# Latent heads: a pair's projection may come one pair sooner, more tiles for its operands, even filling

## The chip, the cores and the metric

The kernel runs on one core of a Trainium2 chip, in one launch. The metric is the device time of an execution in microseconds (us). Five engines work beside each other, each through its own queue and in the order of that queue: TensorE (PE; its weight loads are listed as PEld), VectorE (DVE), ScalarE (ACT), GpSimd (POOL) and SyncE (SP), which here issues nearly all loads.

## The reference, cut

One encoder layer over 512 positions of width 2048, all float32:

```
mod = silu(c) @ w_ada + b_ada                  # six rows: shift, scale, gate, twice
h   = rms_norm(x) * (1 + sc1) + sh1
proj = h @ w_in                                # q, k, v of 8 differential heads; cq (512), ckv (256), k_pe (64)
a   = softmax(q1 k1 + bias) - lam * softmax(q2 k2 + bias)     # per differential head, q and k normed
a_out = rms_norm(a @ v) * (1 - lambda_init)
q_m = rms_norm(rms_norm(cq) @ w_q_b)           # 8 latent heads of 128 + 64, rotary on the 64
kv  = rms_norm(ckv) @ w_kv_b                   # k_nope (128) and v (128) of each latent head
k_m = rms_norm([k_nope, k_pe])                 # rotary on the 64
b_out = softmax(q_m k_m) v
x = x + gt1 * ([a_out, b_out] @ w_out)
x = x + gt2 * ((silu(h2 @ w_gate) * (h2 @ w_up)) @ w_down)    # h2 = second norm and modulation of x
```

## The kernel before

A float32 matmul is done as three matmuls of halves: each operand is split into a high part (`hi`) and a rest (`lo`), and hi·hi, hi·lo and lo·hi are summed in PSUM (L242, L243, L244). Splitting a weight block takes a cast on ScalarE (L90) and a subtraction (L98) on VectorE or on GpSimd, which take turns.

Four stages follow each other: the input modulation and the first part of the input projection (0 to 200 us), the eight differential heads (to 542 us), the eight latent heads (to 755 us), and then the output projection, the second norm and the feed-forward part, whose code the diff leaves alone.

TensorE runs its instructions in the order in which the program is written; a scheduler places those of the other engines around them. The heads are written out step by step by two strings: `DIFF_STEPS` for a differential head, `MLA_STEPS` for a latent one (`s` scores of a block of 128 queries, `t` transposes of the softmax, `v` products with v, `o` operands of the next head, `e` the transposes of a finished head's outputs, `F` filler). At an `F`, `between()` takes matmuls from a generator, `projections()` (L979), for so many microseconds, and a piece of the sums of the modulation (`side`). The numbers are `DIFF_FILL` (per differential head, in eight parts) and `MLA_FILL` (per latent head, in four parts).

`projections()` gives, in this order: the input projection for the later differential heads and for the latents; then for each pair of latent heads `mla_project(pr)` (48 matmuls with `w_q_b`, here QB: L242 to L244 with `cqh`/`cql`, and 24 with `w_kv_b`, KVB: with `ckvh`/`ckvl`); behind pairs 1 and 3 half an output projection, `out_half` (matmuls into `ps_o`). Behind each pair it stops until the first head of this pair has been started and the last differential head's outputs exist (L995). Where it stops, an `F` gives nothing.

What a pair's projection brings along on the other engines: copies of the query tiles out of PSUM (`qm`, L840), sums of squares (L859, L872), and on GpSimd the rotary part of four query tiles (L792 to L795, L854), their statistics (L861 to L863), the key statistics (L880, L261, L262) and eight scalings of key tiles (`kn` L884, `kpt` L886). The last thing a differential head does on GpSimd is four times, for each block of 128 queries, the norm of its output: `zs` (L766 to L768) and `z` (L769). `finish()` transposes the four z on TensorE (L775) at the `e` of the next head; for differential head 7 that is the `e` of latent head 0, behind the first scores of that head.

`dup_tile` gives the tiles for `qpe` and `kpt` (eight buffers: four of each, one pair), `split_v` and `vr` share the tag `v` (eight buffers). `ada` tiles (L308) hold the loads for the modulation's sums; all these loads are issued by SyncE in order.

Of the kernel before, what the change touches and what calls it, by code (L numbers as in the profile page):

```python
# [10 lines left out]
F32 = mybir.dt.float32  # L11
F32R = mybir.dt.float32r
# [6 lines left out]
P = 128  # L19
# [4 lines left out]
H = 8  # L24
# [175 lines left out]
def hybrid_layer(ctx, tc, a, out):  # L200
    nc = tc.nc
# [62 lines left out]
    sh = open_pool("sh")  # L264
# [320 lines left out]
    for i, (k0, nk) in enumerate(BLOCKS):  # L585
        final = i + 1 == len(BLOCKS)
        for h in range(1 if final else FIRST):
            tag = next_tag()
# [20 lines left out]
    wk = open_pool("wk")  # L609
# [13 lines left out]
    def dup_tile(name):  # L623
        return sh[1].tile([P, 2, 2, 64], F32, tag="dup", bufs=8, name=name)

    def split_v(src, own=False):
        vv = (wk if own else sh)[1].tile([P, 2, P], F32R, tag="v", bufs=2 if own else 8, name="v")
        act.copy(out=vv[:, 0, :], in_=src)
        dve.tensor_tensor(out=vv[:, 1, :], in0=src, in1=f(vv)[:, 0, :], op=ALU.subtract)
        return vv  # L630
# [44 lines left out]
    mixT = [None] * KC  # L675
# [166 lines left out]
    def mla_project(pr):  # L842
# [23 lines left out]
        kn, kp, v = [], [], []  # L866
        rk = sm(2 * NT, "rsk", 2)
        for t in range(NT):
            pv = pss[t].rearrange("p (h s n) -> p h s n", h=2, s=2)
            sq = wk[1].tile([P, 384], F32, tag="sq", bufs=2, name="sqm")[:, :256].rearrange("p (a b) -> p a b", a=2)  # L870
            act.activation(sq, pv[:, :, 0, :], AF.Square)
            dve.tensor_reduce(out=rk[:, 2 * t:2 * t + 2], in_=sq, axis=AX.X, op=ALU.add)  # L872
            vr = sh[1].tile([P, 2, P], F32, tag="v", bufs=8, name="vr")
            act.copy(out=vr, in_=pv[:, :, 1, :])
            v.append(vr)
            k = raw_tile("kn")[:, :256].rearrange("p (h n) -> p h n", h=2)
            copy(K_ACT[t], k, pv[:, :, 0, :])
            kn.append(k)
# [101 lines left out]
    def projections():  # L980
# [10 lines left out]
        for pr in range(4):  # L991
            yield from mla_project(pr)
            if pr in (1, 3):
                yield from out_half({1: 2, 3: 3}[pr])
            while pr not in started or mixT[H - 1] is None:  # L995
                yield 0
# [477 lines left out]
DIFF_STEPS = "s0 F s1 n F t0 F e s2 v0 F t1 F s3 v1 F t2 F o0 v2 t3 F o1 v3 F"  # L1474
DIFF_FILL = (26.0, 26.0, 26.0, 26.0, 26.0, 26.0, 26.0, 26.3)
DIFF_SIDE = (1, 2, 1, 2, 1, 2, 1, 1)
# [3 lines left out]
MLA_STEPS = "s0 F t0 e F1 t1 s1 v0 F t2 F1 v1 t3 s2 F v2 F1 o0 v3 F o2 o3 s3 o1 F1"  # L1480
MLA_FILL = (16.0, 15.7, 16.0, 0.2, 14.1, 19.0, 3.3, 12.8)

# [37 lines left out]
```

## Time and profile before

| | |
|---|---|
| median of 3 runs | 2257.24 us (2250.57 to 2259.51) |
| the profiled execution | 2254.27 us, of which its span 2252.5 us |
| mean granted clock of TensorE | 0.996 |
| TensorE busy | 2178.6 us, 97% of the span |
| its weight loads | 2000.5 us, 89% |
| VectorE busy | 1648.1 us, 73% |
| ScalarE busy | 942.6 us, 42% |
| GpSimd busy | 262.7 us, 12% |

All rows below are of the profiled execution, in microseconds from the start of its span. A row of the timeline gives start, duration, engine, line, operation, out<-in and shapes; in brackets how long the engine had been idle before, and what ended that.

### The profile page before, as it was taken

Reading aid. Unit: us, or ns where it says so; the run is one execution under the profiler, and the core shown is the slowest. Engines: PE = TensorE matmul, PEld = TensorE weight load, DVE = VectorE, ACT = ScalarE, POOL = GpSimd, SP = SyncE. Lnnn points to the kernel's source line nnn. Section 1 sums busy time; section 2 is a strip of 40 time slices with the busy share of each in tenths; the row PEclk is TensorE's granted clock in tenths of the full one; section 3 lists DMA queues with packets and bytes.
Section 4 is the critical chain, followed back from the end, with each engine's and each line's share of the span. In section 5 each row is a group of like instructions: output and inputs, shape, how many; then the busy total and the mean of one; then the engine's idle time right before and its main releaser. Section 6 shows DMA issues by size and latency. Waiting matters only on the chain.

```text
span 2252.5 us, 35369 instructions
## 1 busy us (share of the span) xinstructions
PE 2178.6 (97%) x13906; PEld 2000.5 (89%) x13906; DVE 1648.1 (73%) x2362; ACT 942.6 (42%) x1567; POOL 262.7 (12%) x408
## 2 busy tenths in 40 slices
PE   3899999998989999999999999999999999999999
PEld 3899998998777788899999999999999888888887
DVE  5997888868988687867777777777777677443554
ACT  4434555566555334534444444444444522221221
POOL 0003444345554000000000000000000000000000
PEclk9999999999999999999999999999999999999999
DMA  9995355422442684523333333333334686333443
GB/s 284 302 292 169 83 154 158 134 87 86 158 139 96 247 295 159 159 85 118 117 118 117 132 122 122 114 118 116 122 123 131 219 296 224 99 127 99 154 149 103
DMA packets 270826, 345.00 MB, mean 153 GB/s; under 512 B 15005, under 2 KB 171142, under 8 KB 270530
## 3 DMA queue, kind: packets, MB, share of 16 engines
q1 hardware_dynamic: 267864, 338.18, 46.5%
q10 hardware_dynamic: 2794, 4.55, 0.5%
q8 instruction: 109, 1.79, 0.3%
q14 instruction: 59, 0.48, 0.1%
HBM read 322.71 MB, written 19.96 MB: 152 GB/s over the span
## 4 chain that ended last, share of the span: by engine, by line
PE 67%; DVE 1%; DMA 0%; ACT 0%; issue 0%; POOL 0%; SPq 0%; DVEq 0%
PE ps_d L243 7%; PE ps_d L244 7%; PE ps_d L242 7%; PE ps_X L1285 5%; PE ps_X L1283 5%; PE ps_X L1284 5%; PE ps_W L1285 3%; PE ps_W L1283 3%; PE ps_W L1284 3%; PE ps_Y L1285 2%; PE ps_Z L1285 2%; PE ps_o L242 2%; PE ps_o L244 2%; PE ps_o L243 2%; PE ps_Y L1283 2%; PE ps_Z L1283 2%
## 5 line engine op out<-in xcount | busy, mean ns | idle before, releaser
L90 ACT CAST hi<-raw 128x1024 fp32r<-128x1024 f32 (+2 forms) x228 | 221.2, 970 | 479.2 <-PE ps_d L243 262.7
L98 DVE TENSOR_TENSOR lo<-raw,hi 128x1024 fp32r<-128x1024 f32 (+2 forms) x215 | 242.6, 1129 | 217.3 <-ACT hi L90 213.5
L1266 ACT CAST wh<-wr 128x1024 fp32r<-128x1024 f32 x160 | 168.2, 1051 | 245.3 <-PE ps_X L1284 69.2
L1285 PE MATMUL ps_X<-comb,wl 128*128 128x256 f32 x960 | 269.4, 281 | 0.0
L1283 PE MATMUL ps_X<-comb,wh 128*128 128x256 f32 x960 | 268.6, 280 | 0.0
L1284 PE MATMUL ps_X<-comb,wh 128*128 128x256 f32 x960 | 267.1, 278 | 0.0
L1249 DVE TENSOR_TENSOR wl<-wr,wh 128x1024 fp32r<-128x1024 f32 x160 | 195.6, 1222 | 76.5 <-ACT wh L1266 76.2
L244 PE MATMUL ps_d<-lo,ax 128*128 128x512 f32 x640 | 249.0, 389 | 0.0
L243 PE MATMUL ps_d<-hi,ax 128*128 128x512 f32 x640 | 249.0, 389 | 0.0
L242 PE MATMUL ps_d<-hi,ax 128*128 128x512 f32 x640 | 249.0, 389 | 0.0
L242 PE MATMUL ps_in<-hi,hh 128*128 128x384 f32 (+2 forms) x704 | 234.9, 334 | 3.3 <-ACT hh L397 1.3
L243 PE MATMUL ps_in<-hi,hl 128*128 128x384 f32 (+2 forms) x704 | 229.2, 326 | 4.3 <-DVE hl L403 4.3
L244 PE MATMUL ps_in<-lo,hh 128*128 128x384 f32 (+2 forms) x704 | 229.2, 326 | 3.4 <-DVE lo L98 3.4
L1266 ACT CAST wh<-wt 128x1024 fp32r<-128x1024 f32 x120 | 126.4, 1053 | 196.0 <-PE ps_X L1284 118.5
L1249 DVE TENSOR_TENSOR wl<-wt,wh 128x1024 fp32r<-128x1024 f32 x120 | 146.7, 1223 | 80.5 <-ACT wh L1266 80.3
L1283 PEld LDWEIGHTS ps_X<-comb,wh 128*128 128x128 f32 x960 | 180.5, 188 | 0.0
L1284 PEld LDWEIGHTS ps_X<-comb,wh 128*128 128x128 f32 x960 | 180.5, 188 | 0.0
L1285 PEld LDWEIGHTS ps_X<-comb,wl 128*128 128x128 f32 x960 | 180.2, 188 | 0.0
L1285 PE MATMUL ps_W<-comb,wl 128*128 128x256 f32 x640 | 179.6, 281 | 0.0
L1283 PE MATMUL ps_W<-comb,wh 128*128 128x256 f32 x640 | 179.2, 280 | 0.0
L1284 PE MATMUL ps_W<-comb,wh 128*128 128x256 f32 x640 | 178.1, 278 | 0.0
L242 PEld LDWEIGHTS ps_d<-hi,ax 128*128 128x128 f32 x640 | 120.2, 188 | 25.0
(324 smaller groups left out, 5330.6 us busy)
## 6 DMA issues: line engine op xcount, KB each, us to landing
raw<-in_w_down_dram SPq DMA_DIRECT2D x88, 512.0 KB
araw<-in_w_ada_dram SPq DMA_DIRECT2D x80, 512.0 KB
wr<-in_w_gate_dram SPq DMA_DIRECT2D x40, 1024.0 KB
wr<-in_w_up_dram SPq DMA_DIRECT2D x40, 1024.0 KB
ada<-in_w_ada_dram SPq DMA_DIRECT2D x128, 256.0 KB
raw<-in_w_in_dram SPq DMA_DIRECT2D x128, 192.0 KB
raw<-in_w_out_dram SPq DMA_DIRECT2D x32, 512.0 KB
x<-in_w_ada_dram SPq DMA_DIRECT2D x64, 256.0 KB
```

What stands on the lines that cost most here:

```text
L90: nc.scalar.copy(out=hi[:, :n], in_=raw[:, :n])
L98: e.tensor_tensor(out=lo[:, :n], in0=raw[:, :n], in1=hi[:, :n].bitcast(F32), op=ALU.subtract)
L242: pe.matmul(o, ah, bh, start=start, stop=False)
L243: pe.matmul(o, al, bh, start=False, stop=False)
L244: pe.matmul(o, ah, bl, start=False, stop=stop)
L1249: dve.tensor_tensor(out=out, in0=x, in1=y, op=ALU.subtract)
L1266: act.copy(out=hi, in_=src)
L1283: pe.matmul(ps[bk], wh[:, k], c[:, 0], start=first and k == 0, stop=False, skip_group_check=True)
L1284: pe.matmul(ps[bk], wh[:, k], c[:, 1], start=False, stop=False, skip_group_check=True)
L1285: pe.matmul(ps[bk], wl[:, k], c[:, 0], start=False, stop=k == 7, skip_group_check=True)
```

## The change

It has four parts. The generator stops behind pair `pr - 1`'s first head instead of pair `pr`'s: after the projection of pair 0 it goes on at once with pair 1, and a pair's projection may be made while the pair before the one ahead is still at work; only `out_half` waits for the last differential head. `DIFF_FILL` of differential head 7 goes from 26.3 to 35 us, and `MLA_FILL` becomes 11 us for each latent head. `dup_tile` has sixteen buffers instead of eight and the tag `v` twelve instead of eight. The scratch memory for GpSimd's own transfers becomes smaller, which makes room for the tiles; this kernel issues no such transfers.

```
@@ dup_tile, split_v @@
-        return sh[1].tile([P, 2, 2, 64], F32, tag="dup", bufs=8, name=name)
+        return sh[1].tile([P, 2, 2, 64], F32, tag="dup", bufs=16, name=name)
...
-        vv = (wk if own else sh)[1].tile([P, 2, P], F32R, tag="v", bufs=2 if own else 8, name="v")
+        vv = (wk if own else sh)[1].tile([P, 2, P], F32R, tag="v", bufs=2 if own else 12, name="v")
@@ mla_project @@
-            vr = sh[1].tile([P, 2, P], F32, tag="v", bufs=8, name="vr")
+            vr = sh[1].tile([P, 2, P], F32, tag="v", bufs=12, name="vr")
@@ projections @@
             yield from mla_project(pr)
             if pr in (1, 3):
+                while mixT[H - 1] is None:
+                    yield 0
                 yield from out_half({1: 2, 3: 3}[pr])
-            while pr not in started or mixT[H - 1] is None:
+            while pr > 0 and pr - 1 not in started:
                 yield 0
@@ tables @@
-DIFF_FILL = (26.0, 26.0, 26.0, 26.0, 26.0, 26.0, 26.0, 26.3)
+DIFF_FILL = (26.0, 26.0, 26.0, 26.0, 26.0, 26.0, 26.0, 35.0)
-MLA_FILL = (16.0, 15.7, 16.0, 0.2, 14.1, 19.0, 3.3, 12.8)
+MLA_FILL = (11.0,) * H
@@ kernel @@
-    nc = _bacc.Bacc("TRN2", target_bir_lowering=False, num_devices=1)
+    nc = _bacc.Bacc("TRN2", target_bir_lowering=False, num_devices=1, dynamic_dma_scratch_size=1024)
```

TensorE at the end of differential head 7, the first scores of latent head 0 (`ps_s`) and the transposes of the last differential outputs; before:

```order
L242 MATMUL ps_s<-kTh,qTh 128x512
L243 MATMUL ps_s<-kTh,qTl 128x512
L244 MATMUL ps_s<-kTl,qTh 128x512
L919 MATMUL ps_s<-k_6402,q_6394 128x512
L920 MATMUL ps_s<-klo,q_6394 128x512
L775 MATMUL ps_zT<-anti,z 128x128 x4
L242 MATMUL ps_in<-hi,cqh 128x384
L243 MATMUL ps_in<-hi,cql 128x384
```

and now:

```order
L242 MATMUL ps_s<-kTh,qTh 128x512
L243 MATMUL ps_s<-kTh,qTl 128x512
L244 MATMUL ps_s<-kTl,qTh 128x512
L919 MATMUL ps_s<-k_6596,q_6588 128x512
L920 MATMUL ps_s<-klo,q_6588 128x512
L775 MATMUL ps_zT<-anti,z 128x128 x4
L242 MATMUL ps_o<-hi,mh 128x512
L243 MATMUL ps_o<-hi,ml 128x512
```

The 48 QB and 24 KVB matmuls of pair 1, which followed the transposes, now stand ahead of these scores, spread over differential head 7; behind the transposes the first matmuls of `out_half` follow. The other projections of a pair move too, that of pair 3 from latent head 4 to latent head 3, and fewer output matmuls are left behind the last head (65 instead of 86). Behind these output matmuls TensorE's order is the same to the end.

GpSimd behind the last operands of pair 0; before, the four z of differential head 7 follow at once, two of them here:

```order
L884 TENSOR_TENSOR kn<-kn,rsk 128x256
L886 TENSOR_TENSOR kpt<-kpe,rsk 128x256
L766 TENSOR_SCALAR zs<-zs 128x1
L767 TENSOR_TENSOR zs<-zs,cf 128x1
L768 TENSOR_TENSOR zs<-zs,mhalf 128x1
L769 TENSOR_TENSOR z<-z,zs 128x128
L766 TENSOR_SCALAR zs<-zs 128x1
L767 TENSOR_TENSOR zs<-zs,cf 128x1
L768 TENSOR_TENSOR zs<-zs,mhalf 128x1
L769 TENSOR_TENSOR z<-z,zs 128x128
```

and now:

```order
L886 TENSOR_TENSOR kpt<-kpe,rsk 128x256
L98 TENSOR_TENSOR lo<-raw,hi 128x1024
L766 TENSOR_SCALAR zs<-zs 128x1
L767 TENSOR_TENSOR zs<-zs,cf 128x1
L768 TENSOR_TENSOR zs<-zs,mhalf 128x1
L792 TENSOR_TENSOR rt<-qm,qtab 128x2x32
L769 TENSOR_TENSOR z<-z,zs 128x128
L792 TENSOR_TENSOR rt<-qm,qtab 128x2x32
L794 TENSOR_TENSOR qpe<-qm,qtab 128x2x64
L795 TENSOR_TENSOR qpe<-qpe,rt 128x2x64
L854 COPY qpe<-qpe 128x2x64
```

The four z now stand among the steps of pair 1: the first behind one weight split (L98), the second behind the rotary part and the statistics of the queries, the third and the fourth behind the last key scaling of pair 1.

SyncE behind the last key/value weights of pair 0; before:

```order
L74 DMA raw<-in_w_kv_b_dram 128x2x512
L74 DMA raw<-in_w_out_dram 128x2x512 x2
L308 DMA ada<-in_w_ada_dram 128x512 x9
L74 DMA raw<-in_w_out_dram 128x2x512 x2
L308 DMA ada<-in_w_ada_dram 128x512 x8
```

and now:

```order
L74 DMA raw<-in_w_kv_b_dram 128x2x512
L74 DMA raw<-in_w_out_dram 128x2x512 x4
L74 DMA raw<-in_w_q_b_dram 128x2x384
L308 DMA ada<-in_w_ada_dram 128x512 x9
L74 DMA raw<-in_w_q_b_dram 128x2x384
L308 DMA ada<-in_w_ada_dram 128x512 x8
```

Five weight loads, four of the output projection and one of the next pair, now stand ahead of the nine loads for the modulation's sums, where two stood.

## Rows read from the trace of the kernel before

**Rows 1.** Busy time by stretch: length, each engine's us (count), clock, DMA, GB/s.

```profile
200.00:498.00 298.00, 292.30 (x1937) 282.43 (x1936) 244.74 (x515) 161.55 (x395) 132.03 (x206) 1.00 0.45 134
498.00:755.17 257.17, 238.82 (x1223) 198.73 (x1220) 214.36 (x424) 144.45 (x335) 125.48 (x189) 0.97 0.37 119
755.17:2252.50 1497.33, 1490.21 (x9864) 1369.53 (x9862) 1034.38 (x1201) 555.01 (x702) 3.25 (x6) 1.00 0.45 148
546.00:714.50 168.50, 158.87 (x801) 132.65 (x802) 152.26 (x284) 90.26 (x190) 87.69 (x114) 0.98 0.41 133
546.00:755.17 209.17, 198.98 (x1002) 164.09 (x1002) 176.32 (x341) 110.05 (x231) 90.93 (x115) 0.98 0.39 125
676.22:708.02 31.80, 31.47 (x152) 25.36 (x151) 30.37 (x51) 14.43 (x30) 19.79 (x22) 1.00 0.44 147
```

The engines stand in the order PE, PEld, DVE, ACT, POOL in each row; the clock is 1.00 at TensorE's full speed.

**Rows 2.** The same view, three stretches with a low granted clock.

```profile
533.70:540.50 6.80, 5.35 (x26) 5.38 (x27) 5.83 (x13) 2.71 (x8) 5.53 (x11) 0.50 0.73 240
632.70:636.10 3.40, 3.27 (x8) 2.65 (x9) 2.53 (x7) 0.29 (x2) 3.32 (x4) 0.50 0.72 225
649.80:653.10 3.30, 3.30 (x12) 2.93 (x11) 2.27 (x6) 0.00 (x0) 0.00 (x0) 0.50 0.57 152
```

**Rows 3.** The timeline of TensorE around the last differential outputs.

```profile
528.87 0.65 PE L749 MATMUL ps_aT<-ident,pm 128*128 128x128 f32 x4 [0.65 <-DVE ml L638]
...
535.15 1.09 PE L749 MATMUL ps_aT<-ident,pm 128*128 128x128 f32 x4 [3.46 <-DVE cf L735]
...
543.66 0.49 PE L775 MATMUL ps_zT<-anti,z 128*128 128x128 f32 x3
545.90 0.33 PE L775 MATMUL ps_zT<-anti,z 128*128 128x128 f32 x1 [1.75 <-POOL z L769]
545.98 0.42 PE L242 MATMUL ps_in<-hi,cqh 128*128 128x384 f32 x1
...
555.69 0.34 PE L242 MATMUL ps_in<-hi,cqh 128*128 128x384 f32 x1
...
556.73 0.39 PE L242 MATMUL ps_in<-hi,ckvh 128*128 128x512 f32 x1
...
559.50 0.60 PE L903 MATMUL ps_qT<-ident,qm 128*128 128x128 f32 x4
```

**Rows 4.** The timeline of GpSimd in the same place.

```profile
516.76 0.60 POOL L792 TENSOR_TENSOR rt<-qm,qtab 128x64 f32<-128x64 f32 x2 [0.29 <-DVE qm L840]
...
522.36 1.18 POOL L794 TENSOR_TENSOR qpe<-qm,qtab 128x128 f32<-128x128 f32 x1
...
527.90 0.20 POOL L880 TENSOR_TENSOR rsk<-rsk,sskpe 128x8 f32<-128x8 f32 x1 [0.31 <-DVE rsk L872]
...
530.21 0.61 POOL L884 TENSOR_TENSOR kn<-kn,rsk 128x256 f32<-128x256 f32 x1
...
533.06 1.40 POOL L886 TENSOR_TENSOR kpt<-kpe,rsk 128x256 f32<-128x256 f32 x1
...
535.44 0.61 POOL L886 TENSOR_TENSOR kpt<-kpe,rsk 128x256 f32<-128x256 f32 x1
...
538.08 0.22 POOL L766 TENSOR_SCALAR zs<-zs 128x1 f32<-128x1 f32 x1
...
539.30 0.40 POOL L769 TENSOR_TENSOR z<-z,zs 128x128 f32<-128x128 f32 x1
...
552.57 2.67 POOL L98 TENSOR_TENSOR lo<-raw,hi 128x1024 fp32r<-128x1024 f32 x1 [6.72 <-ACT hi L90]
```

**Rows 5.** VectorE's groups from 542.3 to 714.5: busy us, mean ns, idle before.

```profile
L859 DVE TENSOR_REDUCE rsq<-sqm 128x2 f32<-128x384 f32 x12 | 6.4, 544 | 1.3 <-ACT sqm L858 1.3
L840 DVE COPY kn<-ps_in 128x256 f32<-128x256 f32 x12 | 4.9, 410 | 0.0
L872 DVE TENSOR_REDUCE rsk<-sqm 128x2 f32<-128x256 f32 x12 | 4.9, 406 | 0.0
L840 DVE COPY qm<-ps_in 128x384 f32<-128x384 f32 x6 | 3.3, 546 | 0.0
```

## The prediction

> **What bounds the kernel now.** I read the stretches first [rows 1]. From 755 us on TensorE is busy for 1490.2 of 1497.3 us, and the change touches no order there; from 200 to 498 us, in the differential heads, it is busy for 292.3 of 298.0. Only from 498 to 755 us, where the last differential head ends and the eight latent heads run, does it stand for 18.4 us (257.17 less 238.82), at a mean clock of 0.97. Then the clock [rows 2]: three dips to 0.50, which is 1.2 of 2.4 GHz, each after TensorE had stood or while it was standing; work done at half speed there costs half of its busy time, so 2.7, 1.6 and 1.65 us. 18.4 us of waits and about 6 us of slow clock are all that a smoother filling can win: 1.1% of the run.
>
> Third, TensorE's order of time at the worst place [rows 3]. When head 7 has no projection left to run beside it, the transposes of its softmax wait 0.65 and 3.46 us for VectorE, the clock falls, and the last transpose of its outputs (L775) waits 1.75 us for GpSimd's z (L769). Fourth, GpSimd's order of time [rows 4]: from 516.76 to 536.05 us it works without a pause on the operands of pair 0. It is idle half of the stretch, but it takes its queue in order, and at this place that queue is full.
>
> **The change part by part.**
>
> *Tiles and memory.* Sixteen tiles for the rotary and normed operands instead of eight, twelve for v instead of eight. All loads and stores are issued by SyncE and ScalarE, so the smaller scratch for GpSimd's own transfers takes nothing away. In the differential heads the splits of v move up by some places in VectorE's and ScalarE's queues; TensorE waits there for 5.7 us in all now [rows 1], so this moves the time by 3 us at most either way, and I take zero.
>
> *Pair 1 one pair sooner.* Its 48 query matmuls and 24 key/value matmuls move from behind the first scores of latent head 0 to the middle of head 7. They cost TensorE 6 in 1.04 us and 12 in 2.77 us [rows 3], that is 48 x 0.173 + 24 x 0.231 = 13.8 us, the same before and after. What they cover: the two waits for VectorE (0.65 + 3.46) and the 2.7 us of the first dip. Without anything new TensorE would reach the last transposes of head 7 at 543.66 - 4.1 - 2.7 + 13.8 = 550.7 us. The kernel before, when it has done the same work, stands at 545.98 + 13.8 = 559.8 us. So the step is worth 9 us, if nothing new is late.
>
> *What comes along on GpSimd.* Every matmul of a projection brings GpSimd work, and this queue is the one that the step is moved past. In the order before, the four z follow the last operand of pair 0. In the order after, z number 0 to 3 of head 7 are spread among pair 1's work, and the last two stand behind all of it. Priced by the same steps of pair 0 and of the trace [rows 4]: two weight splits of 2.67 = 5.3; the rotary parts of four tiles and the query statistics, from 516.76 to 527.90 less 0.31 of idling = 10.8; the key statistics, 527.90 to 530.21 = 2.3; eight scalings of keys, 530.21 to 536.05 = 5.8; four z of 1.62 (538.08 to 539.70) = 6.5. Sum 30.7 us. GpSimd's order up to the last operand of pair 0 is unchanged, and that ends at 536.05; its inputs for pair 1 are there in time, since TensorE ends that projection near 546 and GpSimd comes to the key statistics, by the same sum, only near 553. So the last z is done at 536.05 + 30.7 = 566.8 us, and TensorE, which can be there at 550.7, waits some 16 us (some of it perhaps already at the first key/value matmuls of pair 1, whose weight split is the first of the two). It goes on at 567.0: not 9 us ahead of the kernel before but 7.2 behind it. After the 3.46 us wait the clock was at half for 5.35 us of work [rows 2]; I charge 2.7 us again. Place of the step: +9.9 us.
>
> Bounds of the 30.7: the sum takes the steps as they were, with one key scaling at 1.40 and one rotary product at 1.18 us beside others of 0.61 [rows 4]. With these two at 0.61 as well it is 0.79 + 0.57 = 1.4 us less, 29.3; with six more of the eight key scalings at 1.40 it is 6 x 0.79 = 4.7 us more, 35.4. I take 30.7, the measured sum of the same steps; at the ends the place costs 8.5 and 14.6 us. That long instruction ran beside VectorE's subtractions. The Trainium skill (SBUF — State Buffer, "SBUF: two separate sides") says that a VectorE operation with two inputs in SBUF and a GpSimd operation exclude each other for a whole instruction; the row of 1.40 us agrees in kind, and by that rule, with VectorE as dense as it is here, the upper end would be the right one.
>
> *Even filling of the latent heads.* Behind that place TensorE stands for 10.2 us (209.17 less 198.98 from 546 to 755 [rows 1]) and loses 3.3 us to the two later dips [rows 2]: 13.5 us that an even 11 us a head can give back, mostly in head 3, which had 0.2 (both dips are there). What limits it is VectorE: it is busy for 152.3 of 168.5 us from 546 to 714.5, 90%, which is where the early sums of the second modulation end [rows 1]. Of this, one projection's share moves ahead: 4 x 0.544 + 4 x 0.410 + 4 x 0.406 + 2 x 0.546 = 6.5 us [rows 5]. The remaining 145.8 us come after 567, since the loads for the sums are queued on SyncE behind five weight loads now instead of two, and the fifth needs a buffer that GpSimd's second weight split frees near 556. With nothing back the early sums end at 714.5 + 9.9 = 724.4, which leaves VectorE 157.4 us for 145.8, 93%; with all 13.5 back 143.9 us, over 100%. One latent head shows 30.37 of 31.80 us, 95.5% [rows 1]. At that share 145.8 us take 152.7, so 4.7 come back, and if VectorE has done 2 us of it while TensorE stands (the softmax of first scores), 143.9 us take 150.7 and 6.7 come back. I take 6.7, half of the 13.5.
>
> *Tail.* 21 output matmuls less are left for after the last head, 21 x 0.231 = 4.9 us, which are only done sooner. From there on the cover is wide.
>
> **Sum.** +9.9 - 6.7 = +3.2 us. The profiled execution took 2254.3 us (span 2252.5 and 1.8 around it), so 2257.5 by it. The median of the runs, 2257.2, lies 3 us above that execution; against the median the forecast is 2260 us, no change that can be measured.
>
> **The rivals.**
>
> *GpSimd is not late (faster).* If its steps for pair 1 take their bare time or its order holds it up less than it looks, so that the last z is there before 551 us, the 9 us stay and half of 13.5 comes on top: 2257.2 - 15.7 = 2241.5 us. For it: GpSimd is busy for 125.5 of 257.2 us only, and spans on it are rough. By the Trainium skill (Perfetto Trace Analysis, "Identifying the Most-Contended Engine") the engine to look at is the one with the highest occupancy, so not this one; that would be this rival's result. Against it: TensorE waits for z already in the trace before [rows 3], and 16 us of the 30.7 would have to go.
>
> *VectorE does not catch up (slower).* While TensorE stands VectorE gets no scores and no loads for the sums, and everything comes at once behind 567 us. If its share there is the 90.4% of before, the 143.9 us take 159.2, so the early sums end at 726.2, 11.7 us later than now: 2269 us; with GpSimd at its upper end 4.7 more: 2274 us. It decides once VectorE's share from there to the end of the early sums is under 143.9/157.4 = 91.4%, where nothing comes back. For it: that is the share of the whole stretch now. Against it: head 3 held it down with its missing filler, and the one even head shows 95.5%.
>
> *The step does nothing.* In the new order pair 1 does stand in head 7; but the waits on GpSimd and on VectorE may only trade places: +9.9 paid and about as much back, 2257 us, inside the forecast's own range, which goes from 2252 (GpSimd at 29.3, all 13.5 back) to 2267 (30.7, nothing back).
>
> **How the numbers follow.** Forecast (place lost on GpSimd, half of it back) 0.60; GpSimd in time 0.14; VectorE behind 0.20; something in the differential heads 0.06. Range: from 2246, which is 2252 less the 3 us of the differential heads and 3 of scatter (the runs of before lie from 2250.6 to 2259.5), to 2273, which takes in nearly all of the second rival and leaves out the first. A measurement of this kernel can tell about 0.5%, 11.3 us, from no change: faster by more 0.13, within 0.67, slower by more 0.20.
>
> **What would show it.** In the changed kernel's trace: TensorE's transposes L775 (now of head 7, before the first output matmuls) idle for 12 to 18 us with GpSimd's z as what ended it, and a dip of the clock behind; no wait for VectorE at the softmax transposes of head 7; GpSimd busy without a pause for some 50 us; no dips of the clock as those at 632.7 and 649.8 us now; VectorE near 95% up to the end of the early sums; TensorE some 3 us later than in the kernel before at the same instruction of the last output matmuls. The forecast is wrong if the wait at L775 is under 6 us, or if TensorE still stands for over 8 us behind it.

## The result

The changed kernel takes 2271.1 us (median of 5 runs, 2264.8 to 2276.2) where the kernel before takes 2255.6 (5 runs, 2250.6 to 2259.5). The ratio is 1.0072, with a 95% interval of 1.0056 to 1.0087: it is slower by 0.7%, more than the 0.5% that can be told from no change. That lies inside the range of 2246 to 2273 us, but the forecast itself, 2260 us and no change, did not come. What came is close to the time of the second rival, 2269 us, which had a chance of 0.20; two of the costs that make it up are in neither of them, as shown below.

The profiled execution of the changed kernel took 2276.15 us (span 2274.4), the longest of its five; that of before, 2254.27. Between these two the difference is 21.9 us, and nearly all of it arises at four places. The table compares the start of the same TensorE work in both traces; matmuls are numbered in TensorE's order, from 0:

| place | before | after | later by | of it new |
|---|---|---|---|---|
| first query matmul of pair 0 | 516.87 | 520.08 | 3.2 | 3.2 |
| last differential outputs transposed, pair 1 projected | 559.8 (545.98 + 13.8) | 569.14 | 9.3 | 6.1 |
| matmul 4064, from which on the order is the same | 759.97 | 773.64 | 13.7 | 4.3 |
| end of the output projection (L296) | 882.72 | 903.22 | 20.5 | 6.8 |
| end of the span | 2252.5 | 2274.4 | 21.9 | 1.4 |

The last 1.4 us lie in the feed-forward part, where the order is the same and single executions differ by several us either way; nothing is read from them.

**The place with the GpSimd queue** came as described. TensorE in order of time, the rows that answer to [rows 3]:

```profile
520.08 0.34 PE L242 MATMUL ps_in<-hi,cqh 128*128 128x384 f32 x1
...
552.05 0.74 PE L756 MATMUL ps_z<-v,aTh 128*128 128x256 f32 x4 [1.20 <-ACT aTh L634]
...
557.13 0.38 PE L775 MATMUL ps_zT<-anti,z 128*128 128x128 f32 x2
567.43 0.47 PE L775 MATMUL ps_zT<-anti,z 128*128 128x128 f32 x1 [9.92 <-POOL z L769]
569.02 0.48 PE L775 MATMUL ps_zT<-anti,z 128*128 128x128 f32 x1 [1.11 <-POOL z L769]
569.14 0.78 PE L242 MATMUL ps_o<-hi,mh 128*128 128x512 f32 x1
```

TensorE stands in front of L775 for 9.92 + 1.11 = 11.0 us, where it stood for 1.75 before [rows 3], and the next output matmul takes 0.78 us, half speed. The waits for VectorE at the softmax transposes (0.65 and 3.46 us before) are gone. GpSimd at the same place, the rows that answer to [rows 4]:

```profile
539.47 2.84 POOL L98 TENSOR_TENSOR lo<-raw,hi 128x1024 fp32r<-128x1024 f32 x1
...
556.02 0.40 POOL L769 TENSOR_TENSOR z<-z,zs 128x128 f32<-128x128 f32 x1
556.38 2.36 POOL L98 TENSOR_TENSOR lo<-raw,hi 128x1024 fp32r<-128x1024 f32 x1
...
565.18 0.61 POOL L886 TENSOR_TENSOR kpt<-kpe,rsk 128x256 f32<-128x256 f32 x1
...
566.98 0.40 POOL L769 TENSOR_TENSOR z<-z,zs 128x128 f32<-128x128 f32 x1
...
568.56 0.40 POOL L769 TENSOR_TENSOR z<-z,zs 128x128 f32<-128x128 f32 x1
```

From the last operand of pair 0 at 539.47 to the last z at 568.96 it works without a pause for 29.5 us. The third z is only done at 567.38, behind the last key scaling of pair 1 (565.18), although TensorE began the product for it at 552.05.

**The stretches** that answer to [rows 1] and [rows 2], in the same columns: the differential heads; head 7 with the latent heads; then, behind the wait, the latent heads to VectorE's last early sum and to the place where TensorE reads the sums; the wait itself; and four pieces with a low clock:

```profile
200.00:498.00 298.00, 289.06 (x1906) 280.01 (x1905) 241.34 (x504) 159.02 (x386) 132.21 (x199) 0.99 0.44 132
498.00:773.65 275.65, 247.36 (x1268) 205.22 (x1267) 216.10 (x433) 148.03 (x344) 122.53 (x197) 0.96 0.35 115
...
569.20:722.20 153.00, 141.49 (x697) 116.23 (x697) 138.14 (x261) 77.99 (x165) 59.09 (x77) 0.96 0.42 137
569.20:731.10 161.90, 150.39 (x741) 123.56 (x741) 143.63 (x274) 83.48 (x176) 61.51 (x78) 0.96 0.40 131
557.50:569.14 11.64, 0.61 (x3) 0.30 (x3) 1.77 (x3) 0.00 (x0) 10.73 (x20) 0.62 0.69 237
569.10:573.90 4.80, 4.80 (x12) 3.83 (x13) 1.40 (x3) 1.45 (x3) 0.00 (x0) 0.50 0.02 3
661.80:665.00 3.20, 3.15 (x11) 2.62 (x12) 3.11 (x5) 3.20 (x8) 3.06 (x8) 0.65 1.03 378
679.40:682.70 3.30, 3.23 (x11) 2.61 (x11) 2.20 (x8) 0.30 (x1) 2.06 (x3) 0.56 0.72 201
854.50:859.50 5.00, 4.92 (x13) 3.85 (x14) 2.21 (x4) 0.00 (x0) 0.00 (x0) 0.50 0.79 237
```

From 498 us to the end of the latent heads TensorE now stands for 28.3 us (275.65 less 247.36), before for 18.4. Behind the transposes VectorE is busy for 138.14 of 153.00 us up to its last early sum, 90.3%, and TensorE stands for 11.5 us there. The 714.5 us of [rows 1] are the place where TensorE reads the sums (L354); up to the same place, now at 731.1 us, VectorE's share is 143.63 of 161.90, 88.7%, below the 90.4% of before. Two dips remain in the latent heads, and there is one at 854 us that the kernel before did not have.

The same 951 matmuls, from the end of the last transposes (with pair 1 projected) to matmul 4064, in the kernel before and in the changed one:

```profile
559.80:759.97 200.17, 189.98 (x951) 155.23 (x949) 166.86 (x324) 104.53 (x221) 87.07 (x112) 0.98 0.41 134
569.14:773.64 204.50, 191.86 (x951) 156.81 (x951) 167.89 (x327) 102.86 (x215) 63.92 (x79) 0.97 0.37 122
```

Within them the standing has moved by one head. Latent heads 3 and 4 (counted from 0), each from its last scores to those of the next, before and now:

```profile
627.52:650.30 22.78, 16.28 (x81) 12.28 (x80) 19.78 (x44) 10.59 (x24) 12.21 (x20) 0.91 0.31 97
650.30:677.67 27.37, 27.12 (x141) 23.80 (x139) 24.79 (x51) 16.98 (x38) 10.99 (x20) 0.95 0.62 190
...
625.68:652.21 26.53, 24.71 (x139) 21.18 (x137) 23.47 (x53) 15.26 (x36) 20.23 (x34) 1.00 0.38 120
652.21:683.91 31.70, 26.77 (x123) 21.91 (x122) 29.08 (x58) 17.06 (x38) 20.34 (x32) 0.89 0.48 160
```

Head 3, which had next to no filler before, is repaired: TensorE stood there for 6.5 us and now stands for 1.8. In head 4 it stood for 0.3 and now stands for 4.9, and both remaining dips lie there.

**The dip at 854 us belongs to a new wait** in the output projection. VectorE and TensorE there, in order of time:

```profile
836.45 0.75 DVE L315 SCALAR_TENSOR_TENSOR adaacc<-x,c_col,adaacc 128x512 f32<-128x512 f32 x1 [4.95 <-DMA x<-in_w_ada_dram]
...
853.31 1.21 DVE L98 TENSOR_TENSOR lo<-raw,hi 128x1024 fp32r<-128x1024 f32 x1
...
854.58 0.80 PE L244 MATMUL ps_o<-lo,mh 128*128 128x512 f32 x1 [4.12 <-DVE lo L98]
```

VectorE waits 4.95 us for a load of the modulation's sums and then works off sums, residuals and weight splits together; a split comes late, and TensorE waits 4.12 us for it and loses about 2.5 more to the clock (half of the 4.92 us of work at 0.50).

### The profile page after: what moved, and what is told of

It is laid out like the page before. It is cut to its first block, busy times and chain, and to the rows that moved or that the text cites. A ratio compares the mean times of both kernels' runs of the same rounds, so it can differ in the third digit from the quotient of the medians.

```text
span 2274.4 us, 35377 instructions
## 1 busy us (share of the span) xinstructions
PE 2184.9 (96%) x13906; PEld 2005.1 (88%) x13906; DVE 1644.8 (72%) x2362; ACT 943.3 (41%) x1567; POOL 260.0 (11%) x408
## 3 DMA queue, kind: packets, MB, share of 16 engines
q8 instruction: 109, 1.79, 0.3%
## 4 chain that ended last, share of the span: by engine, by line
PE 68%; DVE 4%; DMA 1%; issue 1%; ACT 1%; POOL 1%; SPq 0%; ACTq 0%; DVEq 0%; POOLq 0%
PE ps_d L242 7%; PE ps_d L244 7%; PE ps_d L243 7%; PE ps_X L1287 5%; PE ps_X L1285 5%; PE ps_X L1286 5%; PE ps_W L1287 3%; PE ps_W L1285 3%; PE ps_W L1286 3%; PE ps_Z L1287 2%; PE ps_Y L1287 2%; PE ps_Y L1285 2%; PE ps_Z L1285 2%; PE ps_Z L1286 2%; PE ps_Y L1286 2%; PE ps_o L244 2%
## 5 line engine op out<-in xcount | busy, mean ns | idle before, releaser
L98 DVE TENSOR_TENSOR lo<-raw,hi 128x1024 fp32r<-128x1024 f32 (+2 forms) x215 | 242.7, 1129 | 221.1 <-ACT hi L90 220.1
L242 PEld LDWEIGHTS ps_in<-hi,hh 128*128 128x128 f32 x704 | 134.6, 191 | 9.3 <-DVE raw_s L532 1.6
```

The costliest lines, as they stand in the source:

```text
L98: e.tensor_tensor(out=lo[:, :n], in0=raw[:, :n], in1=hi[:, :n].bitcast(F32), op=ALU.subtract)
L242: pe.matmul(o, ah, bh, start=start, stop=False)
```

## The experiments

### The changed kernel once more

The same kernel, run again.

> The changed kernel once more. Its trace has a wait of 4.12 us of TensorE for a weight split (L98 on VectorE) in the output projection near 854 us, with a dip of the clock behind it, 7.3 us in all, that the kernel before does not have. Theory: it belongs to the new order of VectorE's queue there, so it is in this trace again, at 3 us or more, and the time is near 2271 us. Rival: it was an accident of that execution, which was the slowest of five (2276.15 us); then there is no wait over 1 us there and the profiled execution takes about 2276 - 7 = 2269 us or less.

Measured: 2271.9 us, ratio 1.0073 (1.0056 to 1.0091). The wait at L775 is 11.0 us again, and the wait in the output projection is there again, 3.40 us, with the same dip. So both belong to the order of the kernel and not to one execution. At the first query matmul of pair 0 this execution is 1.9 us late instead of 3.2.

### The tiles alone

The kernel before with the tiles of the changed kernel (in `split_v` too) and its scratch:

```
-        return sh[1].tile([P, 2, 2, 64], F32, tag="dup", bufs=8, name=name)
+        return sh[1].tile([P, 2, 2, 64], F32, tag="dup", bufs=16, name=name)
...
-            vr = sh[1].tile([P, 2, P], F32, tag="v", bufs=8, name="vr")
+            vr = sh[1].tile([P, 2, P], F32, tag="v", bufs=12, name="vr")
```

> The kernel before with the tiles and the scratch of the changed one and nothing else (16 dup tiles, 12 of tag v). The prediction took 0, at most 3 us either way. In the changed kernel's trace TensorE comes to the first query matmul of pair 0 at 520.08 us instead of 516.87. Theory: the extra v tiles move VectorE's splits of v ahead of work that TensorE waits for, in the third to fifth differential head, 3 us: 2258 to 2260 us, the first query matmul near 520. Rival: the 3 us are scatter between executions: 2255 to 2256 us, the first query matmul at 517.

Measured: 2257.9 us, ratio 1.0015 (1.0002 to 1.0027), so 0.5 to 6.1 us slower. The first query matmul of pair 0 stands at 517.04, not at 520, so the 3 us at that place are not shown to be the tiles'. One loss is: between matmuls 1100 and 1200, in the input projection, 1.8 us appear, and they appear in the trace of each of the ten kernels with twelve tiles of tag v and in neither of the two others with eight. TensorE there, of this kernel:

```profile
242.18 0.41 PE L242 MATMUL ps_in<-hi,hh 128*128 128x384 f32 x1 [0.58 <-DVE raw_s L532]
...
245.83 0.45 PE L242 MATMUL ps_in<-hi,hh 128*128 128x384 f32 x1 [1.41 <-DVE raw_s L532]
```

and of the kernel before:

```profile
244.82 0.44 PE L242 MATMUL ps_in<-hi,hh 128*128 128x384 f32 x1 [0.36 <-DVE raw_s L532]
```

The additions that free PSUM (L532) stand later in VectorE's queue, behind four splits of v that have moved up ahead of them, and TensorE waits 1.6 us longer for them. But this trace was 0.7 us ahead of the kernel before when it came there and is only 0.2 us behind at pair 0, so what the tiles cost up to that place is not settled. Up to there single executions scatter by more than 3.2 us: the two other kernels with eight tiles stand at 516.06 and 521.01, those with twelve from 517.04 to 524.04.

The larger part lies in the latent heads, where the prediction gave the tiles no term. With TensorE's order that of the kernel before, the same 951 matmuls take 204.5 us instead of 200.2:

```profile
560.04:764.53 204.49, 191.32 (x950) 156.12 (x949) 165.01 (x326) 105.14 (x222) 82.23 (x105) 0.97 0.40 130
```

That is 4.3 us in one trace; the two traces of the changed kernel differ by 1.1 us there. Behind matmul 5000 this execution gained 4 us on that of the kernel before, where nothing was changed, so its whole time hides the loss.

### GpSimd's queue in the other order

The changed kernel with the rotary parts, statistics and key scalings of pair 1 behind the four z of head 7:

```
+        if pr in LATE_POOL:
+            later.append(query_steps)
+        else:
+            query_steps()
...
                     diffs[H - 1].finish()
+                    with tc.issue_after(diffs[H - 1].last):
+                        while later:
+                            later.pop(0)()
```

`LATE_POOL` is (1,), `query_steps` holds the lines L792 to L863 unchanged, `key_steps` is treated likewise, and `last` is the last L769 of a head.

> The changed kernel with one difference in GpSimd's queue: the rotary parts, statistics and key scalings of pair 1 stand behind the four z of differential head 7; all other work is the same. Theory (GpSimd's queue is the cost): the wait for z at L775 falls from 11.0 us to under 3, the dip of the clock behind it goes, and the kernel is 9 to 14 us faster than the changed one: 2257 to 2262 us. Rival (VectorE is the bound, the place does not matter): the wait for z goes as well, but TensorE waits as much more for VectorE in the latent heads behind it: less than 5 us faster than the changed one, 2266 to 2271 us.

Measured: 2262.5 us, ratio to before 1.0031 (1.0018 to 1.0044): 9.4 us faster than the changed kernel on the same chip. TensorE at the last z:

```profile
558.54 0.33 PE L775 MATMUL ps_zT<-anti,z 128*128 128x128 f32 x1 [1.79 <-POOL z L769]
```

and the stretch behind it, up to matmul 4014 and up to matmul 4064, in the columns of the stretches above:

```profile
558.80:750.95 192.15, 178.72 (x900) 147.23 (x899) 164.46 (x314) 98.20 (x205) 83.62 (x112) 0.98 0.37 125
558.63:762.94 204.31, 189.77 (x951) 155.19 (x951) 171.25 (x327) 102.80 (x215) 83.79 (x113) 0.98 0.39 129
```

The wait goes from 11.0 to 1.79 us, the dip behind it goes, and the gain stays: the latent heads behind it take 192.15 us up to matmul 4014, in the changed kernel, whose order of TensorE is the same, 192.49. GpSimd's order is the cost of this place, 9 to 10 us. But the 204.3 us up to matmul 4064 are 4.1 more than the 200.2 of before, so against the kernel before the even filling gave nothing back even without the wait; against the kernel with the tiles alone (204.5) the time is level. The wait in the output projection is still there (3.51 us, 5.3 with the clock).

This run also tests the price of the step itself. With z in time, TensorE needs 39.4 us from the first query matmul of pair 0 (519.27) to the end of the last transposes, where the kernel before needs 42.9 for the same work: the step is worth 3.6 us at its place, with 1.8 us of waiting for z still in it, and not 9.

### Even filling alone

The kernel before with

```
-MLA_FILL = (16.0, 15.7, 16.0, 0.2, 14.1, 19.0, 3.3, 12.8)
+MLA_FILL = (11.0,) * H
```

> The kernel before with the even filling of 11 us for each latent head and nothing else; no projection comes sooner. Theory of the prediction: even filling gives back half of 13.5 us: 2249 us, and the two dips of the clock at 632.7 and 649.8 us are gone. Rival: VectorE sets the pace there and nothing comes back: 2254 to 2258 us, with as many us of waits of TensorE from 546 to 755 us (10.2) as now, only at other places.

Measured: 2277.0 us, ratio 1.0102 (1.0081 to 1.0123), which neither theory had. From the last z to matmul 4014, as many matmuls as before take 228.0 us instead of 202.8, and TensorE stands for 30.3 us of it. The stretch:

```profile
545.80:773.80 228.00, 197.66 (x972) 161.47 (x972) 173.54 (x339) 108.62 (x230) 86.41 (x115) 0.94 0.31 103
```

and TensorE at its worst place:

```profile
657.56 0.48 PE L650 MATMUL ps_k<-ident,kpt 128*128 128x128 f32 x1 [8.91 <-POOL kpt L886]
658.70 0.47 PE L650 MATMUL ps_k<-ident,kpt 128*128 128x128 f32 x1 [0.66 <-POOL kpt L886]
```

With 11 us a head pair 2's projection is done in latent head 3, just ahead of head 4, which needs it, and its operands `kpt` come 9 us late out of GpSimd's queue: 10.9 of the 30.3 us with the waits that follow. With the old uneven numbers it is done in head 2; the filler does not only fill, it decides when the next pair's work begins.

### Pair 1 at its old place, the rest as changed

The changed kernel with

```
-            while pr > 0 and pr - 1 not in started:
+            while mixT[H - 1] is None or pr > 0 and pr - 1 not in started:
...
-DIFF_FILL = (26.0, 26.0, 26.0, 26.0, 26.0, 26.0, 26.0, 35.0)
+DIFF_FILL = (26.0, 26.0, 26.0, 26.0, 26.0, 26.0, 26.0, 26.3)
```

> The changed kernel with pair 1 not in differential head 7: the generator waits behind pair 0 for the last differential outputs as before, head 7's filler is 26.3 us again; the later pairs still come one pair sooner, the filling is an even 11 us. It tells what the step of pair 1 costs or saves by itself. Theory (the step costs what its GpSimd work holds up, about 10 us at that place): no wait over 2 us at L775, and 2260 to 2264 us, about as z_first (2262.5). Rival (the sooner projection of pair 1 is what the even filling lives on): pair 1's work is then missing in latent head 0 and the time is over 2268 us, towards the 2277 us of even filling alone.

Measured: 2277.3 us, ratio 1.0089 (1.0068 to 1.0110). L775 waits 1.75 us, as in the kernel before, and yet the time is that of even filling alone. TensorE at L775:

```profile
553.12 0.33 PE L775 MATMUL ps_zT<-anti,z 128*128 128x128 f32 x1 [1.75 <-POOL z L769]
```

and the stretch behind it, in which it stands for 26 us:

```profile
553.50:776.00 222.50, 196.23 (x972) 160.90 (x970) 170.48 (x336) 106.90 (x227) 86.84 (x115) 0.96 0.33 108
```

So the rival holds: the even filling lives on pair 1 being done in head 7. That step is worth some 6 us as it stands (2277.3 to 2271.1; the intervals of the two overlap) and 15 with GpSimd's queue in the better order (to 2262.5).

### Pair 1 sooner, with the old filling

z_first with the old `MLA_FILL`, and

```
-            while pr > 0 and pr - 1 not in started:
+            while pr > 0 and pr not in started:
```

so that pairs 2 and 3 wait as before.

> The kernel before with the sooner projection of pair 1 alone (35 us of filler in head 7, the tiles), its GpSimd work behind the z of head 7; pairs 2 and 3 come when they came before, and the filling of the latent heads is the old one. Theory (the old filling was fitted to the old places of the projections; sooner projection and even filling belong together): no better than z_first, 2258 to 2266 us. Rival (the sooner pair 1 is worth its 3 to 9 us at the place, and it was the even filling that ate it): 2247 to 2254 us.

Measured: 2278.7 us, ratio 1.0104 (1.0073 to 1.0134), outside both theories and on the side of the first. Latent heads 0 and 1 now get 96 output matmuls in a lump (30 and 66, each head from its last scores to those of the next) and heads 2 to 4 none, where z_first has 21, 51, 24, 0 and 6 in these five. TensorE has single waits for VectorE of 4.93 and 3.91 us at the softmax transposes and takes 212 us instead of 192 for as many matmuls. TensorE:

```profile
588.17 0.47 PE L949 MATMUL ps_aT<-ident,pm 128*128 128x128 f32 x1 [4.93 <-DVE pm L943]
...
647.51 0.48 PE L949 MATMUL ps_aT<-ident,pm 128*128 128x128 f32 x1 [3.91 <-DVE pm L943]
```

The parts of the change only work together: the even filling alone costs 22 us, the sooner pair 1 with the old filling 23.

### The copies of the tiles on ScalarE

z_first and the kernel before, each with

```
-Q_ACT = (0, 0, 1, 1)
-K_ACT = (0, 0, 0, 0)
+Q_ACT = (1, 1, 1, 1)
+K_ACT = (1, 1, 1, 1)
```

so that all of L840 runs on ScalarE.

> The changed kernel with pair 1's GpSimd work behind the z of head 7 (as in z_first, 2262.5 us), and all copies of query and key tiles out of PSUM (L840) on ScalarE instead of VectorE: 4 x 0.41 + 2 x 0.55 = 2.7 us less of VectorE per pair. Theory (VectorE sets the pace of the latent heads; there it is busy for 90.8% with waits of TensorE for it all along): three pairs lie in that stretch, so 4 to 8 us come back: 2254 to 2258 us. Rival (the chain of waits from engine to engine sets it, not VectorE's load): within 3 us of z_first, or slower through ScalarE: 2260 to 2266 us.

> The kernel before with the same copies on ScalarE. Theory (VectorE's load sets the pace of the latent heads in the kernel before as well, 90%): 4 to 8 us faster than before, 2247 to 2251 us. Rival: within 3 us of before, 2252 to 2258 us.

Measured: 2261.6 us for the first (ratio 1.0027, 1.0009 to 1.0045), within 1 us of z_first, and 2259.9 for the second (1.0013, 1.0002 to 1.0025), 0.5 to 5.6 us slower than before. So the rivals hold rather than the theory. But the two decide little: up to matmul 4014 VectorE's busy time fell only from 164.46 to 159.98 us in the first, 4.5 instead of the 8 of the expectation, since the copies of two pairs lie behind the place in z_first, not of three. Up to matmul 4064 that kernel takes 203.8 us instead of 204.3, so these 4.5 us of VectorE are worth 0.5 us in the traces.

### Half of the early sums away from the latent heads

z_first with

```
-MOD_EARLY = 8
+MOD_EARLY = 4
```

> z_first with half of the early sums of the second modulation taken out of the latent heads and done behind them. Only the stretch of the latent heads is read here, from the transposes L775 to matmul number 4014, 192 us in z_first with 164 us of VectorE; the work moved away is some 40 VectorE operations of 0.74 us, 30 us. Theory (VectorE's load sets the pace of that stretch): it gets 8 us shorter or more. Rival (VectorE is only late at the splits of the next head's operands, a chain between TensorE, ScalarE and VectorE that the load does not change): it stays within 4 us of 192. The whole time is not comparable, since the sums come later: 2260 to 2285 us.

Measured: 2270.9 us as a whole (1.0068, 1.0043 to 1.0093), with the sums done later. In two parts, from 655 us on the latent heads have no sums here; and the whole from the last z to the end of the last head's values:

```profile
560.20:655.00 94.80, 88.78 (x465) 74.16 (x464) 85.42 (x160) 51.20 (x110) 61.37 (x94) 1.00 0.37 124
655.00:743.00 88.00, 87.51 (x436) 71.71 (x437) 56.42 (x123) 47.62 (x98) 18.59 (x18) 1.00 0.15 46
559.98:751.32 191.34, 183.72 (x935) 150.88 (x935) 146.51 (x292) 102.55 (x215) 80.18 (x113) 1.00 0.29 95
```

and the second part in z_first, with its sums, and there latent head 4:

```profile
655.00:751.00 96.00, 90.17 (x442) 72.73 (x441) 74.79 (x154) 47.67 (x98) 21.68 (x20) 0.98 0.28 94
641.04:673.39 32.35, 26.78 (x122) 21.93 (x121) 30.05 (x57) 17.09 (x38) 21.79 (x34) 0.89 0.47 158
```

That head here:

```profile
641.45:666.43 24.98, 23.39 (x123) 19.43 (x121) 20.54 (x46) 16.86 (x38) 15.06 (x28) 1.00 0.20 64
```

Matmul 4014 is not the same place in the two kernels, since the 16 matmuls that read a sum (L354) have moved behind it here. To the end of the last head's values z_first takes 204.31 us (its second row above) and this kernel 191.34: 13.0 us less, of which 1.8 are those 16 matmuls. VectorE has 24.7 us less to do there (171.25 less 146.51). In the heads without sums TensorE stands for 0.5 of 88.0 us, in those of z_first with sums for 5.8 of 96.0. Over half of the gain lies in head 4, which goes from 32.35 to 24.98 us: in z_first it holds a pair's projection and sums together, VectorE is busy for 93% of it, and TensorE waits for VectorE's copies out of PSUM and for splits of the next head's operands. So VectorE's sums are what the latent heads wait behind.

### Late weight splits in turns

z_first with VectorE and GpSimd taking turns (`OUT_SPLIT`) in the late output projections too; the end of one line:

```
-OUT_SPLIT if j < 4 and b != 1 else "dve"
+OUT_SPLIT if j < 4 and b != 1 or b > 0 else "dve"
```

> z_first with the weight splits of the late output projections taken in turns by VectorE and GpSimd (which does next to nothing there) instead of by VectorE alone. The new order of VectorE's queue puts one split behind the sums and residuals there: TensorE waits 3.4 to 4.1 us near 850 us in both traces of the changed kernel and in z_first, and with the dip of the clock behind it that is 5.3 us that the kernel before does not have. Theory (the place in VectorE's queue is the cost): that wait falls under 1 us and the kernel is 4 to 6 us faster than z_first, 2256 to 2258 us. Rival (the loads for the sums or the weights are late, whoever splits): the wait stays, 2261 to 2264 us; or GpSimd's 2.7 us for a split makes it late at other places.

Measured: 2262.1 us, ratio 1.0030 (1.0017 to 1.0043): no change. The wait of 3.5 us for VectorE's split is gone, but from matmul 4200 to 4500 TensorE loses 5.4 us against the kernel before all the same, in smaller pieces (0.91 us behind a sum, 0.61 behind a split on GpSimd); z_first loses 6.4 there. So moving the splits does not give the time back. VectorE waits for loads of the sums for 8.5 us in all here, for 10.3 in z_first; whether they are the cause is what the next run tests.

### More output matmuls left for the tail

z_first with

```
-MLA_FILL = (11.0,) * H
+MLA_FILL = (11.0,) * 7 + (6.1,)
```

> z_first (2262.5 us) with 6.1 us of filling instead of 11 in the last latent head, so that 21 output matmuls (4.9 us) are left for after it again, as in the kernel before. In z_first and in the changed kernel only 8.0 us of output matmuls lie between the end of the last head's values and matmul number 4100, in the kernel before 12.8; the loads for the second half of the modulation's sums start once the last head's tiles are free, 9.5 us ahead of matmul 4100 instead of 19.7. Theory (the output projection waits because those loads start too late against it): the 5.3 us near 850 us fall to under 1.5, and the kernel is 3 to 5 us faster than z_first, 2257 to 2260 us. Rival (the wait has nothing to do with what is left for the tail): the last head gets slower or the wait stays, 2261 to 2264 us.

Measured: 2257.9 us, ratio to before 1.0007 (0.9994 to 1.0020): 4.6 us faster than z_first, 5.4 by the ratios, since the two were measured on different chips. In the stretch in which z_first waits TensorE has no gap, here from 835 to 860 us:

```profile
835.00:860.00 25.00, 25.00 (x120) 20.90 (x119) 21.14 (x30) 9.05 (x16) 0.00 (x0) 1.00 0.84 284
```

The loads are what moved. SyncE in the changed kernel, the second load for the late sums (the last row), and VectorE's last split of v ahead of it:

```profile
764.91 0.43 SPq L1133 DMA_DIRECT2D gt<-rowd  x1
772.03 0.28 DVE L629 TENSOR_TENSOR v<-vr,v 128x128 fp32r<-128x128 f32 x1
772.33 0.33 SPq L308 DMA_DIRECT2D x<-in_w_ada_dram  x1
```

and in the kernel before:

```profile
747.92 0.43 SPq L1131 DMA_DIRECT2D gt<-rowd  x1
748.40 0.43 SPq L308 DMA_DIRECT2D x<-in_w_ada_dram  x1
```

It is issued 23.9 us later, while the same output matmul (number 4100) is only 13.7 us later (768.13 and 781.82). It leads that matmul by 19.7 us before, by 9.5 in the changed kernel and in z_first, and by 15.1 in z_first_tail. In the changed kernel SyncE waits 7.0 us ahead of it for VectorE's last split of v (L629, done at 772.31), so it goes out when the last latent head is nearly over; output matmuls that are done ahead of that end are no longer there to cover the loads behind it. The other traces agree: with leads of 13.6 us and more (pair1_first 13.6, tiles_only 14.2, late_start 16.3, even_only 18.3) TensorE has no wait over 0.1 us from matmul 4200 to 4500.

The moved matmuls are only half of it. In the kernel before this load goes out without waiting for the last split, 5 us ahead of it; with the tiles alone it waits 5.7 us for it, and the lead falls from 19.7 to 14.2 us. The output matmuls that moved take the other 4.7. The tiles by themselves do not bring TensorE's wait; the moved matmuls without the tiles were not run.

### The early sums spread evenly

z_first_tail with the early sums at an even 1.27 pieces (`MLA_SUMS`) for each filler of the latent heads until they are done, instead of 1 or 2:

```
-                    between(MLA_FILL[g] / MLA_STEPS.count("F"), MLA_SIDE[i])
+                    at = sums_at[0] + MLA_SUMS
+                    between(MLA_FILL[g] / MLA_STEPS.count("F"), int(at) - int(sums_at[0]))
+                    sums_at[0] = at
```

> z_first_tail (2257.9 us) with the early sums of the second modulation spread over seven latent heads instead of being done after five and a half: 1.27 pieces at each filler instead of 1 or 2 (8.9 a head instead of 11), all else the same. In z_first_mod the latent heads without sums had no wait for VectorE while those with sums kept theirs, 9.2 us in all. Theory (a head's waits grow faster than the sums that VectorE takes up in it, so an even share is cheaper): 3 to 5 us less, 2253 to 2255 us, level with the kernel before or just ahead of it. Rival (each sum costs TensorE the same wherever it stands): 2256 to 2260 us, and the waits only move into the sixth and seventh head.

Measured: 2255.2 us, ratio to before 1.0005 (0.9993 to 1.0017), level with the kernel before. The stretch from the last z to matmul 4014 is 191.2 us against 193.4:

```profile
556.50:747.70 191.20, 176.18 (x900) 145.22 (x899) 163.15 (x317) 97.48 (x206) 80.78 (x112) 0.99 0.39 128
```

The median is 2.7 us below that of z_first_tail, but the two were measured on different chips, and by the ratios to the kernel before (1.0007 and 1.0005) the difference is 0.4 us: a gain in the whole time is not shown. No version beat the kernel before; the change with three of its costs repaired or eased is as fast as that.

## Why the prediction was right and wrong

**Right: the place with the wait.** GpSimd's 30.7 us were 29.5, the last z came at 568.96 instead of 566.8 (pair 0 began 3.2 us later), the reader of L775 stood for 11.0 us. The forecast had 16: TensorE got there at 557.1 instead of 550.7, 3.2 of it from the differential heads, the rest new waits such as the 1.20 us above and some more work than the sum held. The price of the place was 6.1 us and 2.4 for the dip (half of 4.80), 8.5 against the +9.9 forecast, and z_first shows the mechanism: with GpSimd's order turned round the kernel is 9.4 us faster. The upper end of 35.4 us did not come: pair 1's eight key scalings took 0.61 us but for one of 0.79. The lower end was read too high: the trace before has one more long scaling (1.05 us), and the rotary products beside the one of 1.18 take 0.46 and not 0.61, so the bare sum is some 28.7 us, not 29.3. By the Trainium skill (SBUF — State Buffer, "SBUF: two separate sides") a VectorE operation with two inputs in SBUF and a GpSimd operation that reads SBUF exclude each other for a whole instruction. This place does not show what that costs: VectorE waited while the scalings ran, busy for 1.77 of 11.64 us. The first rival, that GpSimd would be in time since it is idle half of the time, is out: the engine with 11% of the span was the one waited for, where the Trainium skill (Perfetto Trace Analysis, "Identifying the Most-Contended Engine") would look at the one with the highest occupancy. Its 2241.5 us would not have come with GpSimd in time either: z_first, where that is so, takes 2262.5, for the step is worth 3.6 us at its place instead of 9, and nothing comes on top.

**Wrong: 6.7 us back from even filling.** This is the step that failed. It took one head at 95.5% of VectorE as the share of an even filling. VectorE's work up to the place where TensorE reads the sums was as forecast, 143.6 us against 143.9; the time that it took was 161.9 us instead of 150.7, a share of 88.7%, under the 91.4% that the second rival named as its point. The stretch behind the transposes takes 204.5 us against 200.2 before; without the 2.4 us of the dip that is 1.9 us more, and in z_first, which has no dip there, 4.1 more, not 6.7 less. The even filling did repair the head that had none, and TensorE then stood in the next one, where a pair's projection and the sums meet. z_first_mod shows what stands in the way, VectorE's sums, which were in the new order as before; even_only and pair1_first show that the filling was never a term by itself: it fixes when each pair's projection is made, and alone it costs 22 us. One cause stays open: the tiles alone lengthen the same stretch by 4.3 us in their one trace, so the rest of the change may have given back 0.2 to 2.4 us there, against a loss that the forecast did not have.

**Wrong: the tail at nothing.** The forecast let 21 output matmuls go from the tail, "only done sooner", with wide cover behind. They were about half of the cover that the late sums' loads lost, the tiles took the other half. It cost 5.3 us in z_first and in the second trace of the changed kernel, 7.3 in the first (matmul 4400 to 4500, against the kernel before), and 4.6 us of the median came back with the one number of z_first_tail.

**The tiles**, taken at zero with 3 us either way for the differential heads alone, cost 0.5 to 6.1 us by themselves. The differential heads were 3.2 and 1.9 us late in the two traces; 1.8 us of loss in each belong to the tiles of tag v, the rest is within what executions scatter there.

By its own test (over 8 us of standing behind L775) the forecast fell: 11.5 us; the dips did not go, and TensorE was 13.7 us later at the start of the last output matmuls and 20.5 at their end, instead of 3. That the time lies in the range is owed to its upper end, which was set for the second rival. That rival's mechanism came, VectorE not catching up. Its time of 2269 us is close by luck: its 11.7 us were the place at 9.9 and the latent heads at 1.8, and it had neither the tail nor the tiles. The sum with the measured terms is 1.8 (tiles) + 8.5 (place) + 1.9 (latent heads) + 5.3 (tail) = 17.5 us; the medians differ by 15.5. The terms are from single traces, and the 1.9 may hold more of the tiles.

## What to carry to other kernels

A step that is moved sooner takes its whole queue entries with it: price the in-order engine that is rarely busy by what stands behind what, as well as the busy ones. Work used as filler has two more roles, it decides when its own successors can start and it covers loads later on; before a sum books moved filler as free, look for what was issued behind the place that it leaves. A share of VectorE that one stretch reached is no forecast for another with other work in it: find out which operations the waits stand behind first. More buffers are an edit of the schedule too: they let work move up in the queues and move the memory that later loads wait for.

## What was not expected of the hardware

A weight split of 1.2 us that comes 3.4 to 4.1 us late costs 5 to 7: TensorE's granted clock fell to 0.50 for 4.92 us of work after the 4.12 us wait, and for 4.80 after the 11.0 us one, so the longer wait had no longer dip. Taking 4.5 us off VectorE by using ScalarE gave 0.5 us of TensorE's time in the latent heads, taking 24.7 us of sums away 13.0 (1.8 of it TensorE's own work).
